# Substitution on 16-blocks, and a 32x32-matmul step to 32-blocks, in an rwkv scan on Trainium2

## The chip, the cores and the metric

One core of one Trainium2 chip runs the whole program. The metric is device time in microseconds (us) of one execution; the figure given for the kernel before is the median of its runs. The engines are PE (TensorE matmuls; PEld is its weight load), DVE (VectorE), ACT (ScalarE), POOL (GpSimd) and SP (SyncE, which here only issues DMAs).

## The reference

Two blocks follow each other on 512 tokens of width 1024. The first mixes a gated linear recurrence with dilated attention. The second has a latent of 512 and a context of 256 tokens; it merges pooling, a differential attention and an rwkv scan, and ends in a mixture of 32 experts. What the change touches is the rwkv scan, which runs over tokens in both directions, for 8 heads of 64:

```
def wkv_step(S, inp):
    r, w, k, v, a, b = inp
    sa = einsum('dbhvk,dbhk->dbhv', S, a)
    S = S * w[..., None, :] + sa[..., None] * b[..., None, :] + v[..., None] * k[..., None, :]
    return S, einsum('dbhvk,dbhk->dbhv', S, r)
```

The context is scanned first, in both directions, and its two final states start the scans of the latent. The expert stage reads 32 experts of three 1024x512 float32 matrices each.

## The kernel before, in words

**The scan in chunks.** The kernel does not step token by token. It takes chunks of 64 tokens. Inside a chunk, the effect of `a` and `b` on later tokens is a triangular 64x64 system for each head, and the inverse of its unit triangular matrix is needed. Between chunks only the 64x64 states are carried. There are 12 chunks (4 of the context, 8 of the latent) and 2 directions. A *batch* is two chunks of one direction, so there are 12 batches, taken alternately from the two directions (line 1319). A batch holds 2 chunks (`s`) x 4 feature tiles (`f`) x 2 heads per tile (`e`), which is 16 systems of 64x64.

**Phases of a batch.** `ph_a` (line 1128, once per chunk) loads the operands, forms decays with scans and exponentials, multiplies them into `AR` and `BK`, and puts the masked products into `AMB`. `ph_i` (line 1178) inverts the two 32x32 diagonal blocks of each of the 16 systems, 32 blocks in all: four DMAs bring the blocks to DRAM (`atD`), one brings them back as `LT`, laid out so that one of 32 blocks lies on each partition and each block is on four partitions. 31 steps of two DVE instructions (lines 1194 and 1196, tiles `Tm` and `Ti`) do the substitution; a partition holds 8 of the 32 rows of the inverse. Four DMAs store the result to `ttD`. `ph_b` (line 1201) loads it back with four DMAs into the diagonal blocks of `TT`, completes the 64x64 inverse with three groups of 32x32 matmuls through the PSUM tile `pi` (lines 1250 to 1262: a transposing matmul to get `T1`, a product `Qs`, a product into the off-diagonal block of `TT`, each evacuated by DVE for one half and ACT for the other), then applies the inverse (`px`, into `XV` or `XW`), forms the operands of the states (`pW`, evacuated into `WW`, lines 1282 to 1292), and carries the states through the two chunks (`pch`, `SI`, lines 1300 to 1312).

**Order.** The program is written as a list of calls; a planner then orders the instructions of each engine ahead of the run by their priorities and by its own estimates of their durations. On the chip each engine executes its list in order, so an instruction that waits holds up whatever is queued behind it on that engine, and this goes for DMA issues on SP too. `batch(n)` calls `ph_a` and `ph_i` of batch n, and then `ph_b` of batch n-2 (lines 1331 to 1338). Between the batches, projections of other branches are called as filler: `rw_prep` of the latent and `gate` in the first four batches, and after them the differential attention's q, k, v projections, the pool branch and more gates. All projections go through `load_chunk` (a DMA issued on SP, line 297, two buffers in this stage) and `split_chunk` (ACT `wh` line 304, POOL `wl` line 305, three buffers).

**Buffers.** PSUM in this stage has two banks for `mm` (projections), three for `aux` (`pta`, `pz0`, `pi`, `px`, and in `rw_prep` the lora products), one for `ch` and two for `pa` (`pA`, `ptb`, `pW`). `WW` has one buffer (`WWB = 1`), so the operands of the second chunk of a batch are written into the same place as those of the first. `AMB` has three buffers.

Of the kernel before, what the change touches and what calls it, by code (L numbers as in the profile page):

```python
# [9 lines left out]
F32 = mybir.dt.float32  # L10
# [3 lines left out]
ALU = mybir.AluOpType  # L14
# [25 lines left out]
def _consts():  # L40
    f = np.float32
    groups, off = {g: [] for g in "012345"}, {}
    where = {"bias1": "1", "invf": "1", "cos2": "3", "sin2": "3", "hsel": "5", "hbc": "5",
             "mask": "2", "tinit": "2", "sgn": "2",
             "iota32": "4", "tokid": "4", "tri": "4", "slot": "4", "tokrow": "4"}
# [59 lines left out]
    ti = np.zeros((4, 32, 8, 32))  # L105
    for g in range(4):
        for q in range(8):
            ti[g, :, q, 4 * q + g] = 1
    add("tinit", ti)
    return {"cst" + g: np.concatenate(v, 1) for g, v in groups.items()}, off  # L110


# [78 lines left out]
def _build(ctx, tc, A, out, dbg, upto):  # L191
# [901 lines left out]
    EARLY = ("kb", "kr", "cs", "ep", "em", "BK", "LT", "Ti", "Tm")  # L1093
# [6 lines left out]
    atD = [dp.tile([2, 2, 8, 32, 32], F32, name="atD%d" % i) for i in range(4)]  # L1100
    ttD = [dp.tile([2, 2, 8, 32, 32], F32, name="ttD%d" % i) for i in range(4)]
    yD = [dp.tile([128, 8, 4, 64], F32, name="yD%d" % d) for d in range(2)]
    par = ((0, E0), (1, E1))
    WWB = 1
    LATB, LPN = 10, (6, 5, 5, 3)

    def w1(name, shape=(4, 64), bufs=1, dt=F32):
# [12 lines left out]
    for d in range(2):  # L1120
        for e in range(2):
            t = rp.tile([128, 4, 64], F32, name="SI%d%d" % (d, e))
            GP.memset(t, 0.0)
            ir = slice(64, 128) if e == 0 else slice(0, 64)
            V.tensor_copy(t[ir], bc(ident[ir, None, ir], [64, 4, 64]))
            SI[d, e] = t

    def ph_a(d, c, s, AMB):

# [45 lines left out]
                          AF.Copy, scale=sgn[:, e:e + 1])  # L1175
        return AR, dec

    def ph_i(d, AMB, bi):

        for e in range(2):  # L1180
            for i in range(2):
                r0 = 64 * e + 32 * i
                SY.dma_start(atD[bi][e, i].rearrange("q s t -> s q t"),
                             AMB[r0:r0 + 32, e, :, :, 32 * i:32 * i + 32].rearrange("p s f t -> p (s f) t"))
        LT = w1("LT", (32, 32), 2)
        SY.dma_start(LT.rearrange("p s t -> p (s t)"),
                     atD[bi].rearrange("e i q s t -> (e i q) (s t)")[None].to_broadcast([4, 32, 1024]))
        T = w1("Ti", (8, 32), 2)
        SC.activation(T, tinit, AF.Copy)
        tmp = w1("Tm", (8, 32))  # L1190
        for s in (range(31) if d == 0 else range(31, 0, -1)):
            js, ts_ = (slice(0, s // 4 + 1), slice(s + 1, 32)) if d == 0 else (slice(s // 4, 8), slice(0, s))
            nj, n = js.stop - js.start, ts_.stop - ts_.start
            V.tensor_tensor(tmp[:, :nj, :n], bc(LT[:, s, None, ts_], [128, nj, n]),  # L1194
                            bc(T[:, js, s:s + 1], [128, nj, n]), ALU.mult)
            V.tensor_tensor(T[:, js, ts_], T[:, js, ts_], tmp[:, :nj, :n], ALU.add)  # L1196
        td = ttD[bi].rearrange("e i q (j g) t -> g (e i q) j t", g=4)
        for g in range(4):
            SY.dma_start(td[g], T[32 * g:32 * g + 32])

    def ph_b(d, chs, sts, AMB, bi):

        lat, c0 = chs[0] >= 4, min(chs)
        XE, XO = XV1 if lat and d else XV
        T = TT[d]
        fs = [(s, f) for s in range(2) for f in range(4)]
# [33 lines left out]
        c1, c2 = slice(32 * d, 32 * d + 32), slice(32 - 32 * d, 64 - 32 * d)  # L1240
        pi = ps("pi", "aux")
        T1, Qs = w1("T1", (2, 4, 32)), w1("Qs", (2, 4, 32))

        def evac(dst, src_):
            V.tensor_copy(dst[0], src_[0])
# [7 lines left out]
        for q, (s, f) in enumerate(fs):  # L1253
            for e in range(2):
                PE.matmul(col(pi, q, 32)[q2[e]], AMB[q1[e], e, s, f, c2], T1[q1[e], s, f, :], start=True,
                          stop=True, tile_position=(q1[e].start, q2[e].start))
        evac([Qs[q2[e]] for e in range(2)], [sf(pi, q2[e], 0, 32) for e in range(2)])
        for q, (s, f) in enumerate(fs):
# [63 lines left out]
    def run_b():  # L1322
        n, sts = pend.pop(0)
        ph_b(*sts)
        if n == 3 and dbg is not None and "S_c" in dbg:
            for d_ in range(2):
                for e, rows in par:
                    SY.dma_start(dbg["S_c"][128 * d_:128 * d_ + 128][rows, 256 * e:256 * e + 256],
                                 SI[d_, e][rows].rearrange("p a b -> p (a b)"))

    def batch(n):
        d, chs = batches[n]
        AMB = w1("AMB", (2, 2, 4, 192), 3)
        sts = {c - min(chs): ph_a(d, c, c - min(chs), AMB) for c in chs}
        ph_i(d, AMB, n % 4)
        pend.append((n, (d, chs, sts, AMB, n % 4)))
        if len(pend) > 2:
            run_b()

# [42 lines left out]
    for n in range(4, 12):  # L1382
        batch(n)
    while pend:
        run_b()
    if upto <= 2:
        return
# [742 lines left out]
```

## Time and profile before

| | |
|---|---|
| median of 3 runs | 1983.2 us (1969.72 to 1985.23) |
| the profiled execution's own time | 1981.57 us |
| its span, first to last instruction | 1979.7 us |
| mean granted TensorE clock | 0.934 |
| PE busy | 1755.4 us (89%) |
| DVE busy | 1091.5 us (55%) |
| ACT busy | 619.1 us (31%) |
| POOL busy | 526.5 us (27%) |

The span is what lies between the first and the last instruction. Busy times of different engines overlap. A busy PE is modelled, and its shares say little about how fast it works; the granted clock is a share of full speed. The scan's stage runs from about 535 us, when the first substitution begins, to about 1160 us. The experts' stage begins at about 1460 us and lasts to the end.

### The profile page before, as it was taken

To read this page: it belongs to the slowest core of one execution; us is meant where nothing else is said; L and a number is where in the kernel's file an instruction comes from. 1 tells how busy PE (TensorE), PEld (TensorE's weight loads), DVE (VectorE), ACT (ScalarE), POOL (GpSimd) and SP (SyncE) were. 2 spreads that over 40 slices of the span, in tenths; PEclk is the share of its full clock that TensorE was granted. 3 is DMA by queue.
4 is the path that set the end of the run, shared out by engine and by line. 5 is a ranking of instruction groups with operands and counts; after the bars stand their busy time and mean duration, and the time that the engine had idled before them with its cause. 6 is when DMAs were issued, how large, how long until landed. Compare 5 with 4: busy or idle time off the path is not lost. (4 is left out here: it accounts for less than half of the span.)

```text
span 1979.7 us, 31352 instructions
## 1 busy us (share of the span) xinstructions
PE 1755.4 (89%) x12309; PEld 1246.3 (63%) x12310; DVE 1091.5 (55%) x2364; ACT 619.1 (31%) x1164; POOL 526.5 (27%) x379
## 2 busy tenths in 40 slices
PE   6899998967787887888879998988979999999998
PEld 3874677953565776677667876677954545444544
DVE  4555675275487746777788655776342333332332
ACT  4234454443443222223333233443221111111110
POOL 2510337442335332231331132642310110101010
PEclk8999998988898898889898999999979999999999
DMA  8336513567546445445355338653629999999998
GB/s 298 108 111 218 197 64 103 195 181 250 156 121 171 135 137 122 109 109 137 99 151 152 81 112 280 204 179 111 246 99 387 387 386 386 386 387 386 386 386 289
DMA packets 275295, 415.89 MB, mean 210 GB/s; under 512 B 104876, under 2 KB 126408, under 8 KB 274888
## 3 DMA queue, kind: packets, MB, share of 16 engines
q1 hardware_dynamic: 246248, 383.44, 58.0%
q10 hardware_dynamic: 25568, 16.78, 2.8%
q0 software_dynamic: 3328, 13.63, 2.4%
q8 instruction: 98, 1.61, 0.3%
q14 instruction: 53, 0.43, 0.1%
HBM read 370.26 MB, written 43.53 MB: 209 GB/s over the span
## 5 line engine op out<-in xcount | busy, mean ns | idle before, releaser
L305 POOL TENSOR_TENSOR wl<-wr,wh 128x1024 fp32r<-128x1024 f32 x125 | 308.3, 2473 | 495.8 <-ACT wh L304 455.5
L304 ACT ACTIVATE wh<-wr 128x1024 fp32r<-128x1024 f32 x125 | 131.6, 1054 | 141.2 <-issue 54.9
L1980 POOL TENSOR_TENSOR yl<-ey,yh 128x512 fp32r<-128x512 f32 x30 | 38.4, 1279 | 466.1 <-ACT yh L1979 466.1
L310 PE MATMUL pf<-h2h,wh 128*128 128x512 f32 x344 | 147.8, 430 | 15.6 <-DVE Ti L1196 10.2
L1194 DVE TENSOR_TENSOR Tm<-LT,Ti 128x60 f32<-128x60 f32 (+24 forms) x372 | 116.8, 314 | 76.9 <-DMA LT<-atD 68.2
L311 PE MATMUL pf<-h2l,wh 128*128 128x512 f32 x344 | 144.5, 420 | 0.0
L312 PE MATMUL pf<-h2h,wl 128*128 128x512 f32 x344 | 143.3, 417 | 0.0
L1974 PE MATMUL ped<-wd,hid 128*64 128x512 f32 (+1 forms) x528 | 127.5, 585 | 0.7 <-ACT hid L1958 0.7
L1935 PE MATMUL peg<-wg,hTg 128*64 128x512 f32 x512 | 126.9, 597 | 0.0
L1942 PE MATMUL peu<-wu,hTg 128*64 128x512 f32 x512 | 125.3, 595 | 0.0
L1196 DVE TENSOR_TENSOR Ti<-Ti,Tm 128x60 f32<-128x60 f32 (+24 forms) x372 | 109.3, 294 | 9.1
L2007 DVE TENSOR_TENSOR acc<-acc,pcb 128x512 f32<-128x512 f32 (+1 forms) x124 | 76.0, 665 | 49.1 <-PE pcb L2006 49.0
L310 PEld LDWEIGHTS pf<-h2h,wh 128*128 128x128 f32 x344 | 69.4, 202 | 38.4 <-issue 15.4
L1974 PEld LDWEIGHTS ped<-wd,hid 128*64 128x64 f32 x528 | 39.9, 136 | 70.6 <-issue 65.9
L1942 PEld LDWEIGHTS peu<-wu,hTg 128*64 128x64 f32 x512 | 43.2, 137 | 65.1 <-issue 62.9
L311 PEld LDWEIGHTS pf<-h2l,wh 128*128 128x128 f32 x344 | 68.8, 200 | 18.5 <-issue 3.4
L1935 PEld LDWEIGHTS peg<-wg,hTg 128*64 128x64 f32 x512 | 41.9, 137 | 60.9 <-issue 58.1
L312 PEld LDWEIGHTS pf<-h2h,wl 128*128 128x128 f32 x344 | 68.6, 199 | 18.2 <-issue 2.1
L1282 PE MATMUL pW<-AMB,XV 128*128 128x64 f32 (+1 forms) x256 | 45.2, 335 | 28.7 <-DVE XV L1271 16.9
L1979 ACT ACTIVATE yh<-ey 128x512 fp32r<-128x512 f32 x30 | 18.9, 630 | 163.6 <-DVE ey L1978 90.2
L1915 DVE TENSOR_SCALAR hTg<-pg,gs,sh 128x128 f32<-128x128 f32 x64 | 25.3, 408 | 75.1 <-PE peu L1942 38.4
L1912 ACT ACTIVATE hTg<-pg,sh,gs 128x128 f32<-128x128 f32 x64 | 28.2, 457 | 121.4 <-PE peu L1942 55.4
(961 smaller groups left out, 4475.1 us busy)
## 6 DMA issues: line engine op xcount, KB each, us to landing
wg<-in_w_exp_gate_dram SPq DMA_DIRECT2D x64, 1024.0 KB
wu<-in_w_exp_up_dram SPq DMA_DIRECT2D x64, 1024.0 KB
wd<-in_w_exp_down_dram SPq DMA_DIRECT2D x62, 1024.0 KB
wr<-in_w_in_dram SPq DMA_DIRECT2D x97, 512.0 KB
kb<-kbD SPq DMA_DIRECT2D x24, 384.0 KB
wr<-in_w_out_dram SPq DMA_DIRECT2D x16, 512.0 KB
LT<-atD SPq DMA_DIRECT2D x12, 512.0 KB
thD<-mth ACTq DMA_DIRECT2D x24, 256.0 KB
```

Of the source, the lines that this page charges most:

```text
L304: SC.activation(hi, raw, AF.Copy)
L305: GP.tensor_tensor(lo, raw, hi.bitcast(F32), ALU.subtract)
L310: PE.matmul(p, ah, bh, start=start, stop=False)
L311: PE.matmul(p, ah, bl, start=False, stop=False)
L312: PE.matmul(p, al, bh, start=False, stop=stop)
L1194: V.tensor_tensor(tmp[:, :nj, :n], bc(LT[:, s, None, ts_], [128, nj, n]), bc(T[:, js, s:s + 1], [128, nj, n]), ALU.mult)
L1196: V.tensor_tensor(T[:, js, ts_], T[:, js, ts_], tmp[:, :nj, :n], ALU.add)
L1282: PE.matmul(pw[e][:, nw * f:nw * (f + 1)], X[:, s, f, :], AMB[:, e, s, f, n0:192], start=True, stop=True)
L1935: mm = PE.matmul(pg[64 * a:64 * a + 64, :], hT[:, k, 64 * a:64 * a + 64], gp[a][k // 4][:, k % 4, :], start=(k == 0), stop=(k == 7), tile_ ...
L1942: PE.matmul(pu[64 * a:64 * a + 64, :], hT[:, k, 64 * a:64 * a + 64], up[a][k // 4][:, k % 4, :], start=(k == 0), stop=(k == 7), tile_posit ...
L1974: PE.matmul(pd[64 * a:64 * a + 64, :], hid[:, m * k + 64 * a:m * k + 64 * a + 64], dn[q][a][:, k, 0:q1 - q0], start=(k == 0), stop=(k == 3 ...
L2007: V.tensor_tensor(acc[i][:, qs], acc[i][:, qs], p, ALU.add)
```

## The change

In `ph_i` the substitution is done on 16x16 diagonal blocks: 64 blocks in a batch, one on each partition and each block on two partitions, 15 steps instead of 31, and rows of 16 elements instead of 32. Eight DMAs instead of four take the blocks to DRAM, one DMA brings them back (1 KB per partition, before 4 KB), two instead of four store the result, and eight load it into the diagonal 16-blocks of a new tile `U` (three buffers, zeroed once). These loads are issued in `ph_i`; those of `ph_b` into `TT` are gone.

A new function `ph_m` joins two 16-blocks to a 32-block by four groups of 32 matmuls of 32x32: the transpose of `U`; the product of the `AMB` block with it, masked by `join` to the one off-diagonal 16-block; and the two products that give the off-diagonal part of the inverse and of its transpose. It uses two PSUM tiles of `aux`, one ACT evacuation and six DVE instructions. `ph_b` gets the transpose `T1` from it and no longer forms it with matmuls and evacuations. `ph_m` of a batch is called one batch later, after `ph_i` of the next batch, and ahead of the `ph_b` of the batch before it. `WW` gets two buffers.

```diff
+    join = cc("join").rearrange("p (d j) -> p d j", d=2)
+    eye = cc("eye32")
+    atD = [dp.tile([2, 4, 8, 16, 16], F32, name="atD%d" % i) for i in range(4)]
+    ttD = [dp.tile([2, 4, 8, 16, 16], F32, name="ttD%d" % i) for i in range(4)]
-    WWB = 1
+    WWB = 2
...
-    def ph_i(d, AMB, bi):
+    def ph_i(d, AMB, U, bi):
         for e in range(2):
-            for i in range(2):
-                r0 = 64 * e + 32 * i
+            for i in range(4):
+                r0 = 64 * e + 16 * i
                 SY.dma_start(atD[bi][e, i].rearrange("q s t -> s q t"),
-                             AMB[r0:r0 + 32, e, :, :, 32 * i:32 * i + 32].rearrange("p s f t -> p (s f) t"))
+                             AMB[r0:r0 + 16, e, :, :, 16 * i:16 * i + 16].rearrange("p s f t -> p (s f) t"))
-        LT = w1("LT", (32, 32), 2)
+        LT = w1("LT", (16, 16), 2)
...
-        for s in (range(31) if d == 0 else range(31, 0, -1)):
-            js, ts_ = (slice(0, s // 4 + 1), slice(s + 1, 32)) if d == 0 else (slice(s // 4, 8), slice(0, s))
+        for s in (range(15) if d == 0 else range(15, 0, -1)):
+            js, ts_ = (slice(0, s // 2 + 1), slice(s + 1, 16)) if d == 0 else (slice(s // 2, 8), slice(0, s))
             nj, n = js.stop - js.start, ts_.stop - ts_.start
             V.tensor_tensor(tmp[:, :nj, :n], bc(LT[:, s, None, ts_], [128, nj, n]),
                             bc(T[:, js, s:s + 1], [128, nj, n]), ALU.mult)
             V.tensor_tensor(T[:, js, ts_], T[:, js, ts_], tmp[:, :nj, :n], ALU.add)
-        td = ttD[bi].rearrange("e i q (j g) t -> g (e i q) j t", g=4)
-        for g in range(4):
-            SY.dma_start(td[g], T[32 * g:32 * g + 32])
+        td = ttD[bi].rearrange("e i q (j g) t -> g (e i q) j t", g=2)
+        for g in range(2):
+            SY.dma_start(td[g], T[64 * g:64 * g + 64])
+        for e in range(2):
+            for i in range(4):
+                r0, c0 = 64 * e + 16 * i, 16 * (i % 2)
+                SY.dma_start(U[r0:r0 + 16, :, c0:c0 + 16], ttD[bi][e, i].rearrange("q j t -> j q t"))
+
+    def b32(p, o, lhs, rhs):
+        for q in range(8):
+            for e, i, r in blocks:
+                PE.matmul(p[r, o + 32 * q:o + 32 * q + 32], lhs(r, q, e, i), rhs(r, q, e, i), start=True, stop=True,
+                          tile_position=(r.start, r.start))
+
+    def ph_m(d, AMB, U):
...
+        pt = ps("tit", "aux")
+        b32(pt, 0, lambda r, q, e, i: U[r, q], lambda r, q, e, i: eye[r])
+        T = w1("T16", (8, 32), 2)
+        SC.activation(T, q8(pt[:, 0:256]), AF.Copy)
+        b32(pt, 256, at, lambda r, q, e, i: T[r, q])
+        P = w1("PJ", (8, 32))
+        V.tensor_tensor(P, q8(pt[:, 256:512]), bc(join[:, d, None, :], [128, 8, 32]), ALU.mult)
+        pu = ps("tiu", "aux")
+        b32(pu, 0, lambda r, q, e, i: P[r, q], lambda r, q, e, i: U[r, q])
+        b32(pu, 256, lambda r, q, e, i: U[r, q], lambda r, q, e, i: P[r, q])
+        for e, i, r in blocks:
+            V.tensor_tensor(TT[d][r, :, :, 32 * i:32 * i + 32], U[r].rearrange("p (s f) t -> p s f t", s=2),
+                            pu[r, 0:256].rearrange("p (s f t) -> p s f t", s=2, f=4), ALU.add)
+        V.tensor_tensor(T, T, q8(pu[:, 256:512]), ALU.add)
+        return T
...
-        for e in range(2):
-            for i in range(2):
-                r0 = 64 * e + 32 * i
-                SY.dma_start(T[r0:r0 + 32, :, :, 32 * i:32 * i + 32].rearrange("p s f t -> p (s f) t"),
-                             ttD[bi][e, i].rearrange("q j t -> j q t"))
...
-                PE.matmul(col(pi, q, 32)[q1[e]], T[q1[e], s, f, c1], ident[q1[e], q1[e]], start=True, stop=True,
-                          tile_position=(q1[e].start, q1[e].start))
-        evac([T1[q1[e]] for e in range(2)], [sf(pi, q1[e], 0, 32) for e in range(2)])
...
+    def join_b():
+        for z in pend:
+            if len(z[1]) == 4 and (len(pend) == 1 or z is not pend[-1]):
+                d, _, _, AMB = z[1]
+                z[1] += (ph_m(d, AMB, U16[z[0] % 3]),)
...
+        ph_i(d, AMB, U16[n % 3], n % 4)
+        pend.append([n, (d, chs, sts, AMB)])
+        if len(pend) > 1:
+            join_b()
         if len(pend) > 2:
             run_b()
...
     while pend:
+        join_b()
         run_b()
```

## Rows read from the trace of the kernel before

**Rows 1.** Stage windows: length, then busy us by engine, granted clock, DMA share, GB/s

```profile
535.00:880.00 345.00, 292.28 (x2265) 231.25 (x2266) 243.22 (x617) 111.44 (x195) 120.04 (x105) 0.87 0.49 128
880.00:1130.00 250.00, 209.41 (x2590) 181.41 (x2590) 196.55 (x620) 82.03 (x164) 58.09 (x58) 0.90 0.48 126
1130.00:1200.00 70.00, 67.55 (x527) 53.12 (x521) 26.62 (x40) 22.81 (x36) 21.23 (x20) 0.98 0.47 152
...
1460.00:1980.00 520.00, 505.19 (x2658) 250.10 (x2657) 170.16 (x339) 67.37 (x129) 38.38 (x30) 0.99 0.99 364
```

**Rows 2.** Who waited for whom, DVE, 535 to 1130 us: total, times, longest

```profile
DVE Tm L1194 <- DMA LT<-atD: 68.2, 10, 11.0
...
DVE WW L1289 <- PE pch L1302: 3.0, 3, 1.6
DVE WW L1289 <- PE pch L1308: 2.0, 2, 1.6
```

**Rows 3.** Who waited for whom, PE, 535 to 880 us

```profile
PE px L1268 <- DVE TT L1245: 15.3, 3, 6.5
PE pf L310 <- DVE Ti L1196: 10.2, 2, 8.0
```

**Rows 4.** Who waited for whom, PE, 880 to 1130 us

```profile
PE pW L1282 <- ACT WW L1292: 19.7, 4, 6.5
PE pW L1282 <- DVE XV L1271: 9.7, 2, 6.9
```

**Rows 5.** The tile Ti: its instructions (ns min/median/max), and their busy sum by windows

```profile
L1194 DVE TENSOR_TENSOR Tm<-LT,Ti x372: 152/214/5960, 535.2 to 1124.5; 128x60 f32<-128x60 f32 x18, 128x54 f32<-128x54 f32 x12, 128x66 f32<-128x66 f32 x12, 128x28 f32<-128x28 f32 x12
L1196 DVE TENSOR_TENSOR Ti<-Ti,Tm x372: 127/212/5912, 538.2 to 1124.7; 128x60 f32<-128x60 f32 x18, 128x54 f32<-128x54 f32 x12, 128x66 f32<-128x66 f32 x12, 128x28 f32<-128x28 f32 x12
...
sum 1500.00, DVE 226.08 ACT 4.89; mean DVE 15.07 ACT 0.33
```

**Rows 6.** DVE and POOL in order of time: start, us, engine, line, what

```profile
916.60 0.20 DVE L1194 TENSOR_TENSOR Tm<-LT,Ti 128x35 f32<-128x35 f32 x1
...
918.63 0.17 DVE L1194 TENSOR_TENSOR Tm<-LT,Ti 128x16 f32<-128x16 f32 x1
...
884.96 2.30 DVE L1196 TENSOR_TENSOR Ti<-Ti,Tm 128x30 f32<-128x30 f32 x1
...
884.87 2.34 POOL L305 TENSOR_TENSOR wl<-wr,wh 128x1024 fp32r<-128x1024 f32 x1 [0.19 <-ACT wh L304]
```

**Rows 7.** DVE groups by shape, 500 to 1200 us: busy, mean ns, idle before

```profile
L1166 DVE TENSOR_TENSOR AMB<-pA,cst 128x256 f32<-128x256 f32 x16 | 6.3, 417 | 9.6 <-PE pA L1162 9.6
...
L1245 DVE COPY T<-pi 32x256 f32<-32x256 f32 x12 | 5.0, 413 | 3.6 <-PE pi L1250 3.4
```

**Rows 8.** ACT and PE in order of time

```profile
917.08 0.38 ACT L1443 ACTIVATE dk<-pt 128x256 f32<-128x256 f32 x1
...
937.14 0.69 PE L1250 MATMUL pi<-cst,TT 32*32 32x32 f32 x32
...
950.97 0.56 PE L1260 MATMUL pi<-TT,Qs 32*32 32x32 f32 x22
```

**Rows 9.** SP in order of time, DMA issues

```profile
913.76 2.07 SPq L1183 DMA_DIRECT2D atD<-AMB  x4
...
917.16 0.58 SPq L1186 DMA_DIRECT2D LT<-atD  x1
...
920.29 7.97 SPq L1199 DMA_DIRECT2D ttD<-Ti  x4
...
930.63 1.80 SPq L1213 DMA_DIRECT2D TT<-ttD  x4
...
963.27 0.56 SPq L1186 DMA_DIRECT2D LT<-atD  x1
```

**Rows 10.** Who waited for whom, 880 to 1130 us, SP and POOL

```profile
SPq L1213 <- DMA ttD<-Ti: 15.5, 8, 7.7
...
POOL wl L305 <- DMA TT<-ttD: 29.0, 1, 29.0
```

More of the change, by code (lines that the diff above doesn't have):

```diff
@@ L43, in _consts @@
     where = {"bias1": "1", "invf": "1", "cos2": "3", "sin2": "3", "hsel": "5", "hbc": "5",
-             "mask": "2", "tinit": "2", "sgn": "2",
+             "mask": "2", "tinit": "2", "join": "2", "eye32": "2", "sgn": "2",
              "iota32": "4", "tokid": "4", "tri": "4", "slot": "4", "tokrow": "4"}
@@ L104, in _consts @@
     add("sgn", sg)
-    ti = np.zeros((4, 32, 8, 32))
-    for g in range(4):
+    ti = np.zeros((2, 64, 8, 16))
+    for g in range(2):
         for q in range(8):
-            ti[g, :, q, 4 * q + g] = 1
+            ti[g, :, q, 2 * q + g] = 1
     add("tinit", ti)
+    jn = np.zeros((4, 32, 2, 32))
+    jn[:, 16:, 0, :16] = 1
+    jn[:, :16, 1, 16:] = 1
+    add("join", jn)
+    add("eye32", np.tile(np.eye(32), (4, 1)))
     return {"cst" + g: np.concatenate(v, 1) for g, v in groups.items()}, off
@@ L1092, in _build @@
     rpa, rpb = (cur["ctx"].enter_context(tc.tile_pool(name=n, bufs=1, reuse_waits="tile")) for n in ("b2i", "b2j"))
-    EARLY = ("kb", "kr", "cs", "ep", "em", "BK", "LT", "Ti", "Tm")
+    EARLY = ("kb", "kr", "cs", "ep", "em", "BK", "LT", "Ti", "Tm", "T16", "PJ")
     load_cst("2", cp2)
@@ L1099, in _build @@
     CW = 0.5 * math.exp(-0.5)
-    atD = [dp.tile([2, 2, 8, 32, 32], F32, name="atD%d" % i) for i in range(4)]
-    ttD = [dp.tile([2, 2, 8, 32, 32], F32, name="ttD%d" % i) for i in range(4)]
+    join = cc("join").rearrange("p (d j) -> p d j", d=2)
+    eye = cc("eye32")
+    atD = [dp.tile([2, 4, 8, 16, 16], F32, name="atD%d" % i) for i in range(4)]
+    ttD = [dp.tile([2, 4, 8, 16, 16], F32, name="ttD%d" % i) for i in range(4)]
     yD = [dp.tile([128, 8, 4, 64], F32, name="yD%d" % d) for d in range(2)]
     par = ((0, E0), (1, E1))
-    WWB = 1
+    WWB = 2
     LATB, LPN = 10, (6, 5, 5, 3)
@@ L1126, in _build @@
             SI[d, e] = t
+    U16 = []
+    for i in range(3):
+        t = rp.tile([128, 8, 32], F32, name="U16%d" % i)
+        GP.memset(t, 0.0)
+        U16.append(t)
     def ph_a(d, c, s, AMB):
@@ L1176, in ph_a @@
         return AR, dec
-    def ph_i(d, AMB, bi):
+    blocks = [(e, i, slice(64 * e + 32 * i, 64 * e + 32 * i + 32)) for e in range(2) for i in range(2)]
+    fs = [(s, f) for s in range(2) for f in range(4)]
+    def ph_i(d, AMB, U, bi):
         for e in range(2):
-            for i in range(2):
-                r0 = 64 * e + 32 * i
+            for i in range(4):
+                r0 = 64 * e + 16 * i
                 SY.dma_start(atD[bi][e, i].rearrange("q s t -> s q t"),
-                             AMB[r0:r0 + 32, e, :, :, 32 * i:32 * i + 32].rearrange("p s f t -> p (s f) t"))
-        LT = w1("LT", (32, 32), 2)
+                             AMB[r0:r0 + 16, e, :, :, 16 * i:16 * i + 16].rearrange("p s f t -> p (s f) t"))
+        LT = w1("LT", (16, 16), 2)
         SY.dma_start(LT.rearrange("p s t -> p (s t)"),
-                     atD[bi].rearrange("e i q s t -> (e i q) (s t)")[None].to_broadcast([4, 32, 1024]))
-        T = w1("Ti", (8, 32), 2)
+                     atD[bi].rearrange("e i q s t -> (e i q) (s t)")[None].to_broadcast([2, 64, 256]))
+        T = w1("Ti", (8, 16), 2)
         SC.activation(T, tinit, AF.Copy)
-        tmp = w1("Tm", (8, 32))
-        for s in (range(31) if d == 0 else range(31, 0, -1)):
-            js, ts_ = (slice(0, s // 4 + 1), slice(s + 1, 32)) if d == 0 else (slice(s // 4, 8), slice(0, s))
+        tmp = w1("Tm", (8, 16))
+        for s in (range(15) if d == 0 else range(15, 0, -1)):
+            js, ts_ = (slice(0, s // 2 + 1), slice(s + 1, 16)) if d == 0 else (slice(s // 2, 8), slice(0, s))
             nj, n = js.stop - js.start, ts_.stop - ts_.start
@@ L1196, in ph_i, with at, q8, ph_b @@
             V.tensor_tensor(T[:, js, ts_], T[:, js, ts_], tmp[:, :nj, :n], ALU.add)
-        td = ttD[bi].rearrange("e i q (j g) t -> g (e i q) j t", g=4)
-        for g in range(4):
-            SY.dma_start(td[g], T[32 * g:32 * g + 32])
-    def ph_b(d, chs, sts, AMB, bi):
+        td = ttD[bi].rearrange("e i q (j g) t -> g (e i q) j t", g=2)
+        for g in range(2):
+            SY.dma_start(td[g], T[64 * g:64 * g + 64])
[9 more added lines that the diff above has]
+    def ph_m(d, AMB, U):
+        def at(r, q, e, i):
+            return AMB[r, e, fs[q][0], fs[q][1], 32 * i:32 * i + 32]
+        def q8(ap):
+            return ap.rearrange("p (q t) -> p q t", q=8)
+        pt = ps("tit", "aux")
[13 more added lines that the diff above has]
+        return T
+    def ph_b(d, chs, sts, AMB, T1):
         lat, c0 = chs[0] >= 4, min(chs)
@@ L1205, in ph_b @@
         T = TT[d]
-        fs = [(s, f) for s in range(2) for f in range(4)]
         v3 = vTD[:, c0:c0 + 2].rearrange("t c (f e v) -> e t (c f) v", f=4, e=2)
@@ L1239, in ph_b @@
         q2 = [slice(64 * e + 32 - 32 * d, 64 * e + 64 - 32 * d) for e in range(2)]
-        c1, c2 = slice(32 * d, 32 * d + 32), slice(32 - 32 * d, 64 - 32 * d)
+        c2 = slice(32 - 32 * d, 64 - 32 * d)
         pi = ps("pi", "aux")
-        T1, Qs = w1("T1", (2, 4, 32)), w1("Qs", (2, 4, 32))
+        Qs = w1("PJ", (2, 4, 32))
         def evac(dst, src_):
@@ L1249, in ph_b @@
             for e in range(2):
-                PE.matmul(col(pi, q, 32)[q1[e]], T[q1[e], s, f, c1], ident[q1[e], q1[e]], start=True, stop=True,
-                          tile_position=(q1[e].start, q1[e].start))
-        evac([T1[q1[e]] for e in range(2)], [sf(pi, q1[e], 0, 32) for e in range(2)])
-        for q, (s, f) in enumerate(fs):
-            for e in range(2):
-                PE.matmul(col(pi, q, 32)[q2[e]], AMB[q1[e], e, s, f, c2], T1[q1[e], s, f, :], start=True,
+                PE.matmul(col(pi, q, 32)[q2[e]], AMB[q1[e], e, s, f, c2], T1[q1[e], q], start=True,
                           stop=True, tile_position=(q1[e].start, q2[e].start))
@@ L1334, in batch @@
         sts = {c - min(chs): ph_a(d, c, c - min(chs), AMB) for c in chs}
-        ph_i(d, AMB, n % 4)
-        pend.append((n, (d, chs, sts, AMB, n % 4)))
+        ph_i(d, AMB, U16[n % 3], n % 4)
+        pend.append([n, (d, chs, sts, AMB)])
+        if len(pend) > 1:
+            join_b()
         if len(pend) > 2:
```

## The prediction, made before the changed kernel ran

> **What bounds the kernel now.** I read the stages first [rows 1]. From 1460 us on the expert stage keeps PE busy for 505 of 520 us at a granted clock of 0.99 and the DMA engines at 0.99: nothing there is touched, and it can only start sooner. From 1130 to 1200 us PE is busy for 67.55 of 70 us. The scan's stage lies before that, and it looks different. In 880 to 1130 us DVE is busy for 196.55 of 250 us (79%), in 535 to 880 us for 243.22 of 345 (70%), while PE stands idle for 250 - 209.41 = 40.6 us and 345 - 292.28 = 52.7 us, at clocks of 0.90 and 0.87. So 93.3 us of PE idleness lies in the scan, and each us of it that goes should show at the end, since what follows starts when the scan's tiles are given back.
>
> Then I asked who makes PE wait. In both windows the long waits are on evacuations: `px` on DVE's copy into `TT` (15.3 us), a projection queued behind the substitution itself (10.2) [rows 3], `pW` on ACT's `WW` and on DVE's copy into `XV` (19.7 and 9.7) [rows 4]. The evacuations are late because DVE's list interleaves them with the substitution. The substitution is the largest single user of DVE: 744 instructions, 226.1 us [rows 5]. DVE itself mainly waits on one thing, `LT` (68.2 us in 10 waits) [rows 2]. A batch takes 963.27 - 917.16 = 46.1 us from one `LT` load to the next [rows 9], so 880 to 1130 us holds 5.4 batches, and the other 6.6 lie before or at the edges.
>
> **The change part by part.** *The substitution.* It falls from 62 to 30 instructions per batch, 744 to 360 in all. Their mean is now 226.1 / 744 = 0.304 us, their median about 0.213 [rows 5]. The new ones are 8 to 36 elements wide, and rows of such widths show 0.17 to 0.20 us [rows 6]; I take 0.18. The difference of mean and median, 0.091 us, comes from a few long ones. One took 2.30 us where its width asks 0.18, and POOL's `wl` split ran from 884.87 to 887.21, just across it [rows 6]. I let the long ones fall with the count: 360 x (0.18 + 0.091) = 97.6 us. The bounds are 360 x 0.18 = 65 us (none of them hit) and 360 x 0.304 = 109 us (they cost today's mean).
>
> The Trainium skill ("SBUF — State Buffer", the section "Who interferes with whom") says that a DVE instruction with two SBUF inputs and a GpSimd one that reads SBUF exclude each other, the later one blocking until the first ends. By that rule the long instructions are POOL's doing and not the substitution's, and the blocking may pass to another DVE instruction rather than fall with the count. It is the second case below.
>
> *The join on DVE.* `ph_m` adds six instructions per batch that read PSUM (the mask, four sums, the sum into `T`). The nearest rows are 0.417 us for 128x256 with a PSUM input and 0.413 for 32x256 [rows 7], so 6 x 0.417 x 12 = 30.0 us. `T1`'s copy goes: 12 x 0.413 = 5.0 us. DVE is left with 226.1 - 97.6 - 30.0 + 5.0 = 103.5 us less, 8.6 per batch (bounds 92 and 136 in all).
>
> *What of it reaches the end.* In 880 to 1130 us 5.4 x 8.6 = 46 us of DVE go. DVE is nearly the pace there but partly waits, so I take 60%: 28 us, under the 40.6 us that PE has to give. In the 6.6 other batches 57 us go; there the latent's projections and their splits also set the pace, and I take 40%: 23 us, under 52.7. Together 51 us. Late next is PE.
>
> *The join on PE.* 128 matmuls of 32x32 come per batch and 16 go: 1344 more. Such matmuls run at 0.69 / 32 = 22 ns apiece, once at 0.56 / 22 = 25 ns [rows 8]: 29 to 34 us. Part fills idle PE; about a third should not: 10 us (bounds 0 and 34). The join's ACT evacuation stands for that of `T1`, some 0.38 us each [rows 8]: nothing.
>
> *Two buffers of `WW`.* With one, DVE's `WW` for the second chunk waits for `pch` of the first: 3.0 + 2.0 us [rows 2]. I count 5 us. The 19.7 us that PE waits on ACT's `WW` [rows 4] look like the same thing, but `pW` waits for a PSUM bank of `pa`, of which there are still two; they are the upper bound (25 us together), zero is the lower.
>
> *DMAs on SP.* Four more stores to `atD`, four more loads back, two fewer stores to `ttD`: six issues of 0.45 to 0.52 us per batch [rows 9], about 3 us, 35 in all. On the way to `LT` lie only the four extra stores, 2.1 us. Against them `LT` brings 128 KB instead of 512: 384 KB take 3.0 us at the 126 GB/s of that window, 1.1 at the 364 GB/s of the last [rows 1]. Between 1.0 us lost and 0.9 won per batch I take nothing, and 12 us either way for the range. The loads into `U` move from `ph_b` to `ph_i`, behind the stores that they read. In the queue they already stand there: `TT`'s loads follow 2 us after `ttD`'s stores end [rows 9]. `ph_m` comes a batch later and has about 46 us of cover; without it, PE would see the wait for the stores, 15.5 / 8 = 1.9 us [rows 10], and four issues more.
>
> *Sum.* 51 - 10 + 5 = 46 us. The profiled execution took 1981.6 us, 1.6 less than the median, so 1981.6 - 46 + 1.6 = 1937 us.
>
> **The rivals.** *The blocking stays.* POOL's work is the same, so the 226.1 - 744 x 0.213 = 67.6 us of long instructions pass to others. DVE then saves only 158.5 - 65 - 25 = 69 us, and the 51 become 34: 34 - 10 + 5 = 29 us, 1954 us. For it speaks the pair of rows at 884.9 us; against it, that many other DVE instructions of this stage read PSUM. It is what the rule named above would have.
>
> *The join's hand-offs hold PE.* `ph_m` passes four times between PE and an evacuation, in two more tiles of the three `aux` banks. Today `px` behind `pi` waited three times, 5.1 us each [rows 3]. If six of the batches get one such wait, 31 of the 46 us go: 1968 us. Ten would give 1988. Against it speaks that `ph_m` does not hang on the states and can lie between projections.
>
> *The SP queue becomes the wait: slower.* After the substitution SP holds the stores (7.97 us in one batch), the 1.9 us until they land and eight loads of 0.45: 13.5 us, in which no projection weight can be issued. POOL once waited 29.0 us for a weight behind a `TT` load [rows 10]. It decides where the hold outlasts the chunks in stock; if half of the hold shows on PE in all batches, 81 us are added: 1937 + 81 = 2018 us. Against it: the stores and loads already stand together, and the two longest PE waits of either window are not on weights [rows 3, 4].
>
> *All idleness goes.* If PE loses its 93.3 us, 1981.6 - 93 = 1888 us, with the joins' matmuls paid by a clock nearer the 0.98 of the next window.
>
> *The second buffer does nothing*, because the bank decides: 5 us less, inside the first case.
>
> **How the numbers follow.** The forecast has 0.42 (its own range 1915 to 1958), the blocking 0.20, the hand-offs 0.18, the SP queue 0.13, all idleness 0.07. A measurement of this kernel can tell about 1%, 20 us, from no change. Below 1963 lie the forecast, the blocking and the full gain, less 0.03 for their edges: 0.66 faster. Within 1%: 0.18 + 0.03 = 0.21. Slower: 0.13. The range runs from 1888 to 1990 us: the full gain below, the hand-offs in ten batches above; most of the SP case and a little at each edge stay out.
>
> **What would show it.** The substitution's busy time should be 65 to 110 us in 360 instructions; well above that, the blocking was mis-sized. DVE's share in the scan's second half should fall from 79% to under 70% while batches come every 39 to 42 us instead of 46. The joins' groups of 32 matmuls should take 0.7 us, and PE should name `tit` or `tiu` in few waits; many, and the hand-offs have it. `TT` and `XV` waits of PE should halve; `WW`'s should stay if the bank decides. Projections that wait on `wl` behind `U`'s loads would show the SP case. I am wrong if batches still come every 46 us with DVE relieved: then something else, in the list's order or in the DMA round trip to `LT`, sets the pace.

## The result, and the profile after

The changed kernel takes **2007.2 us** (median of 4 runs, 2004.5 to 2013.0), against 1984.2 us for the kernel before in the same comparison: ratio **1.0141, 95% interval 1.0098 to 1.0184**, slower by 1.4%. The forecast was 1937 us, 2.3% faster.

First the stage windows of the changed kernel (columns as in [rows 1]), with one row more, from 480 us to the first scores matmul behind the scan:

```profile
535.00:880.00 345.00, 301.84 (x3539) 239.28 (x3538) 183.68 (x421) 103.29 (x185) 110.71 (x97) 0.85 0.45 115
880.00:1130.00 250.00, 209.22 (x3353) 182.82 (x3352) 148.22 (x409) 74.63 (x150) 61.90 (x60) 0.88 0.43 111
1460.00:1980.00 520.00, 497.83 (x2641) 247.17 (x2639) 176.44 (x359) 74.14 (x141) 45.12 (x33) 0.98 0.98 360
480.00:1231.00 751.00, 650.30 (x8263) 530.82 (x8263) 417.64 (x992) 236.06 (x433) 226.85 (x214) 0.88 0.44 118
```

And the last of these rows for the kernel before, whose scores begin 25 us earlier:

```profile
480.00:1206.00 726.00, 614.51 (x5575) 496.97 (x5576) 494.23 (x1316) 239.35 (x433) 225.21 (x211) 0.89 0.51 136
```

The whole loss lies in this stage: 751 - 726 = 25 us, and the spans differ by 2004.0 - 1979.7 = 24.3. In it DVE lost 77 us of work, as the change means it to, and PE's busy time grew by 36 us. PE's idle time, 111.5 us before, is still 100.7: DVE was relieved and PE hardly noticed.

The substitution of the changed kernel by its tile (columns as in [rows 5]) came out as forecast, 96.43 us of DVE in 360 instructions, where 97.6 were worked out:

```profile
L1211 DVE TENSOR_TENSOR Tm<-LT,Ti x180: 150/188/5095, 528.7 to 1141.9; 128x30 f32<-128x30 f32 x36, 128x14 f32<-128x14 f32 x24, 128x24 f32<-128x24 f32 x24, 128x15 f32<-128x15 f32 x12
...
sum 1500.00, DVE 96.43 ACT 3.60; mean DVE 96.43 ACT 3.60
```

But the batches do not come faster. The loads of `LT` in SP's order of time, changed kernel: four batches in 1084.77 - 876.40 = 208.4 us, 52.1 us each, where [rows 9] had 46.1:

```profile
876.40 0.53 SPq L1203 DMA_DIRECT2D LT<-atD  x1
...
1084.77 0.56 SPq L1203 DMA_DIRECT2D LT<-atD  x1
```

Over all 12 loads, from the first to the last (the two times behind the durations), it is 605 us against 567 for the kernel before:

```profile
L1203 SPq DMA_DIRECT2D LT<-atD x12: 528/532/581, 523.4 to 1128.8; - x12
```

```profile
L1186 SPq DMA_DIRECT2D LT<-atD x12: 556/557/613, 523.2 to 1090.5; - x12
```

Who waited for whom on DVE, 535 to 1130 us of the changed kernel (as [rows 2]). The wait for `LT` fell from 68.2 to 30.7 us (40.5 if the window runs on to 1200 us, where the last batch of the changed kernel lies), and what is late now comes mostly from PE:

```profile
DVE BK L1170 <- PE ptb L1185: 37.5, 9, 12.3
DVE WW L1330 <- PE pW L1323: 32.2, 19, 5.7
DVE Tm L1211 <- DMA LT<-atD: 30.7, 9, 6.3
```

The same on PE, 480 to 1231 us. The `pW` waits of [rows 4] are not among them any more; `pi` waits in their place, for `Qs` (in the buffers of `PJ`, from ACT) and for the `T` that `ph_m` leaves:

```profile
PE pi L1301 <- ACT PJ L1292: 24.6, 6, 7.9
PE pi L1296 <- DVE T L1250: 15.6, 5, 4.9
PE px L1309 <- DVE TT L1291: 9.9, 3, 8.8
PE tit L1226 <- DMA U<-ttD: 7.0, 8, 3.0
```

### The profile page after: what moved, and what is told of

It reads as the page before. It is cut to its first block, busy times and chain, and to the rows that moved or that the text cites. A ratio compares the mean times of both kernels' runs of the same rounds, so it can differ in the third digit from the quotient of the medians.

```text
span 2004.0 us, 36536 instructions
## 1 busy us (share of the span) xinstructions
PE 1787.5 (89%) x14997; PEld 1275.4 (64%) x14998; DVE 1012.5 (51%) x2040; ACT 616.4 (31%) x1164; POOL 528.2 (26%) x382
## 5 line engine op out<-in xcount | busy, mean ns | idle before, releaser
L317 PE MATMUL pf<-h2l,wh 128*128 128x512 f32 x344 | 149.1, 433 | 0.0
L2058 DVE TENSOR_TENSOR acc<-acc,pcb 128x512 f32<-128x512 f32 (+1 forms) x124 | 75.8, 665 | 40.5 <-PE pcb L2057 40.3
L1211 DVE TENSOR_TENSOR Tm<-LT,Ti 128x15 f32<-128x15 f32 (+4 forms) x180 | 55.9, 311 | 45.4 <-DMA LT<-atD 40.5
L317 PE MATMUL pt<-wl,h2h 128*128 128x256 f32 x192 | 61.1, 318 | 0.0
L316 PE MATMUL pt<-wh,h2h 128*128 128x256 f32 x192 | 60.6, 315 | 0.3 <-DVE dql L1525 0.3
```

The lines of the kernel that those rows point to most:

```text
L316: PE.matmul(p, ah, bh, start=start, stop=False)
L317: PE.matmul(p, ah, bl, start=False, stop=False)
L2058: V.tensor_tensor(acc[i][:, qs], acc[i][:, qs], p, ALU.add)
```

## Experiments

Ratios are to the kernel before, with 95% intervals; where two other kernels are compared, the difference of their ratios is taken times 1983 us. An edit also lets the planner order the remaining instructions anew. Run 8 shows what a new order alone can do: 3 to 4 us in the kernels without the join, 25 to 27 us in the changed kernel.

**1. DVE's relief alone** (`sub15`). 15 of the 31 steps; the rest of each 32-block's inverse is left out.

```diff
-        for s in (range(31) if d == 0 else range(31, 0, -1)):
+        for s in (range(15) if d == 0 else range(31, 16, -1)):
```

> The kernel before with only 15 of the 31 steps of each substitution (the other 16 steps are left out, so the inverse is incomplete); joins, DMAs and buffers as before. DVE loses 384 of 744 substitution instructions, about 110 us of its 226. Theory H (PE's own issue time and the hand-offs between engines set the scan's pace, DVE's load does not): PE's idle time between 480 us and the first scores falls by less than 20 us, the time stays within 1% of before, 1965 to 2000 us. Theory R (DVE's relief is worth the 51 us that was predicted, and the change loses it and more elsewhere): 1930 to 1945 us.

Measured: 1973.1 us, 0.996 [0.9938, 0.9982]. In the stage DVE fell from 494 to 391 us, a relief as large as the one on which the forecast rests, and 8 us came of it. DVE's share was not the pace.

**2. The same with a smaller `LT`** (`sub15_small_lt`).

```diff
-                     atD[bi].rearrange("e i q s t -> (e i q) (s t)")[None].to_broadcast([4, 32, 1024]))
+        LT = w1("LT", (256,), 2)
+        SY.dma_start(LT, atD[bi].rearrange("e i q s t -> (e i q) (s t)")[None, :, 0:256].to_broadcast([4, 32, 256]))
...
-            V.tensor_tensor(tmp[:, :nj, :n], bc(LT[:, s, None, ts_], [128, nj, n]),
+            V.tensor_tensor(tmp[:, :nj, :n], bc(LT[:, None, 8 * (s % 16):8 * (s % 16) + n], [128, nj, n]),
```

> The kernel before with 15 of the 31 substitution steps, as in the run of that alone, and LT loaded with 1 KB per partition instead of 4 KB, of which the steps read arbitrary overlapping pieces (a part of the inverse is left out, and what is computed is of no use). The number of instructions and their shapes stay those of the run with 15 steps, which gave 1973.1 us and in which DVE waited 100.9 us for LT in 12 waits (8.4 per batch; 36.4 in 11 in the kernel without the join). If the round trip of LT is what held the relief back, the waits fall to about 40 us and the time to 1915 to 1940 us (0.966 to 0.979). If it is hidden by other work, 1965 to 1980 us (0.991 to 0.999), and the gain of the kernel without the join comes from something else.

Measured: **1906.1 us, 0.9648 [0.9608, 0.9687]**: (0.996 - 0.9648) x 1983 = 62 us from a load of 128 KB in place of 512; count and shapes of the instructions are those of run 1. DVE's wait for `LT`, 480 to 1200 us, first with 15 steps alone, then with the small load:

```profile
DVE Tm L1194 <- DMA LT<-atD: 100.9, 12, 11.5
```

```profile
DVE Tm L1193 <- DMA LT<-atD: 23.6, 10, 6.3
```

The first row shows where the relief of run 1 went: the shorter substitution was followed by a longer wait, 100.9 us where there had been 68.2. The two differ by 77.3 us, and the stage is 58 us shorter (PE busy 606.22 of 713 us against 590.33 of 655):

```profile
480.00:1193.00 713.00, 606.22 (x5568) 494.98 (x5567) 391.37 (x927) 234.52 (x428) 221.86 (x209) 0.89 0.52 138
```

```profile
480.00:1135.00 655.00, 590.33 (x5575) 480.44 (x5576) 400.34 (x932) 238.54 (x433) 230.08 (x214) 0.93 0.53 147
```

**3. The change without the join** (`no_join`). `ph_m` without matmuls: `T` by a DVE transpose, `TT` a copy of `U`; the off-diagonal 16-blocks of the inverse are left at zero.

```diff
-        b32(pt, 0, lambda r, q, e, i: U[r, q], lambda r, q, e, i: eye[r])
...
+        V.transpose(T.rearrange("p q t -> p (q t)"), U.rearrange("p q t -> p (q t)"))
...
+            V.tensor_copy(TT[d][r, :, :, 32 * i:32 * i + 32], U[r].rearrange("p (s f) t -> p s f t", s=2))
```

> The changed kernel with the join's matmuls left out: the off-diagonal 16-blocks stay zero, TT gets a DVE copy of U and T1 a DVE transpose of it. Short substitution, its DMAs and two buffers of WW stay. Theory H (the join's matmuls and their hand-offs on PE are what the change loses; the second WW buffer is its only real gain, about 28 us, and the short substitution gives about 8): 1984 - 28 - 8 and a few us for the transposing matmuls that are gone, 1935 to 1955 us. Rival D (the new DMAs or the new plan of the other instructions cost, not the join): 1975 us or more.

Measured: **1913.7 us, 0.9691 [0.9642, 0.9741]**, 61 us faster than the kernel before. The rest of the change is a clear gain, and the join costs (1.0141 - 0.9691) x 1983 = **89 us**. The stage row, and four batches in 946.50 - 810.05 = 136.5 us, 34.1 each:

```profile
480.00:1142.00 662.00, 590.00 (x5188) 479.65 (x5186) 407.58 (x980) 231.40 (x417) 231.29 (x217) 0.91 0.50 139
```

```profile
810.05 0.55 SPq L1203 DMA_DIRECT2D LT<-atD  x1
...
946.50 0.53 SPq L1203 DMA_DIRECT2D LT<-atD  x1
```

Against the changed kernel's stage, 89 us longer, PE is busy 60 us longer and idle 29 us longer. Of the 60 us, the join's matmuls are 44.3 (each row's time until the next one starts or it ends itself, summed over `tit` and `tiu`); the rest is other work at a granted clock of 0.88 instead of 0.91.

**4. One buffer of `WW`**, with the join (`one_ww`) and without it (`no_join_one_ww`; the same blocks at zero).

```diff
-    WWB = 2
+    WWB = 1
```

> The changed kernel with one buffer of WW again. If the second buffer frees only DVE and the PSUM banks of pW decide: within 6 us of the changed kernel, 2001 to 2013 us. If it carries a gain that the joins hide: 15 to 30 us slower than changed, 2020 to 2037 us.

> no_join (join's matmuls left out, the off-diagonal 16-blocks stay zero) with one buffer of WW. If the second buffer is worth the same here as in the changed kernel (28 us): 1936 to 1950 us. If it pays only where the joins crowd PE and the short substitution alone is what gains: within 10 us of no_join, 1905 to 1924 us. If the gain of no_join is nearly all the buffer's: 1965 to 1985 us.

Measured: 1.0287 [1.0237, 1.0337] and 0.9669 [0.9638, 0.97]. The second buffer is worth 29 us with the join and nothing without it. The forecast's 5 us describe neither. What it takes away are DVE's waits for `pch`, as the prediction had it: with one buffer and the join, 480 to 1251 us,

```profile
DVE WW L1330 <- PE pch L1349: 30.7, 6, 8.4
...
DVE WW L1330 <- PE pch L1343: 9.0, 3, 4.9
```

and none with two. Without the join the same waits of the one buffer are 11.5 and 6.8 us, and cost nothing at the end.

**5. The join twice** (`join_twice`): each of its four groups is issued twice.

```diff
-        for q in range(8):
+        for q in list(range(8)) * 2:
```

> The changed kernel with each group of the join's 32x32 matmuls issued twice into the same place (same values), 128 more matmuls per batch; hand-offs, DVE and DMAs as changed. Theory H: PE's issue time adds up in full, the four groups cost about 44 us of PE now, so 30 to 50 us more than the changed kernel, 2037 to 2057 us. Rival W (only the hand-offs of the join cost, the matmuls fill PE's idle time): under 12 us more, 2005 to 2019 us.

Measured: 1.0588 [1.0535, 1.0642], 89 us for the second copy, as much as the first had cost. The second copy adds no evacuation and no PSUM tile, so neither is needed for the price, and its own issue is 32 us (`tit` and `tiu` 76.6 instead of 44.3). PE's idle time in the stage grows by 49 us; 21.8 us of it stand before `tiu` with no wait that the trace shows.

**6. The join issued, but read by nothing** (`join_unread`, `join_unread_after_b`): the kernel of run 3 with the four groups on `U`, `AMB` and the identity, called ahead of `ph_b` and behind it.

```diff
+        pt, pu = ps("tit", "aux"), ps("tiu", "aux")
+        b32(pt, 0, lambda r, q, e, i: U[r, q], lambda r, q, e, i: eye[r])
+        b32(pt, 256, at, lambda r, q, e, i: U[r, q])
+        b32(pu, 0, lambda r, q, e, i: U[r, q], lambda r, q, e, i: U[r, q])
+        b32(pu, 256, lambda r, q, e, i: U[r, q], at)
```

> no_join with the four groups of 32 join matmuls issued again, but on U, AMB and the identity alone and with nothing reading their results: PE's issue time of the join without its hand-offs (the join itself stays left out, the off-diagonal 16-blocks are zero). The changed kernel is 93 us above no_join. If issue time and clock are the price: 60 to 90 us above no_join, 1975 to 2005 us. If the hand-offs through ACT and DVE are: 30 to 50 us above, 1944 to 1964 us.

> The kernel without the join (off-diagonal 16-blocks of the inverse left at zero) with the join's four groups of matmuls issued on other data and read by nothing, as before, but the groups called behind the applying phase of the older batch instead of ahead of it. Called ahead they cost 121 us over the kernel without them (2034.6 against 1913.7). If the place in PE's list is what makes them dear (the older batch's chain of small products stands behind 128 matmuls), 1955 to 1975 us: 40 to 60 us over the kernel without them, near the 44 to 46 us of their own issue, with PE's wait of pi on the evacuation into PJ (46.2 us in 8) gone. If their issue in this stage is dear wherever it stands, 2015 to 2035 us.

Measured: 1.0297 [1.0264, 1.0329] and 1.0314 [1.0274, 1.0353], so 120 and 124 us over run 3. A price made only by the join's hand-offs, or only by the place of the call, is refuted: matmuls that nobody reads cost no less, in either place. The stage rows, ahead and behind, show 66.5 and 82.1 us more of PE work than run 3, of which 46.4 and 44.6 are the groups themselves, at a clock of 0.88 and 0.84, and 58.5 and 57.9 us more of idleness:

```profile
480.00:1267.00 787.00, 656.51 (x8263) 541.17 (x8264) 416.34 (x980) 234.33 (x421) 235.23 (x218) 0.88 0.43 120
```

```profile
480.00:1282.00 802.00, 672.06 (x8263) 551.44 (x8264) 400.20 (x980) 235.13 (x421) 234.65 (x218) 0.84 0.43 117
```

**7. Half the join's matmuls** (`join_dve_t`, and with the call behind `ph_b`, `join_dve_t_after_b`): DVE transposes in place of the first group and of one of the two last ones.

```diff
+        V.transpose(T.rearrange("p q t -> p (q t)"), U.rearrange("p q t -> p (q t)"))
...
-        b32(pu, 0, lambda r, q, e, i: P[r, q], lambda r, q, e, i: U[r, q])
...
+            V.transpose(TT[d][r, :, :, 32 * i:32 * i + 32], T[r].rearrange("p (s f) t -> p s f t", s=2))
```

> The changed kernel with two of the join's four matmul groups and its ACT evacuation replaced by DVE transposes of 32x32 blocks (one of 128x256, four of 32x256); one PSUM tile instead of two. PE loses about 22 us of issue time, DVE keeps its count. Theory H: 15 to 30 us less than the changed kernel, 1977 to 1992 us. Rival W (hand-offs cost): one hand-off to PE and back less per batch, but DVE ones in their place, 1995 to 2010 us.

> The changed kernel with two of the four join groups and their evacuations replaced by DVE transposes, and the join called behind the applying phase of the older batch. The two edits alone gave 1981.8 us (0.9992) and 1980.1 us (1.0014) against 2007 for the changed kernel. If the join's price has two separate parts, the number of matmuls that PE issues (half of them gone, about 25 us) and the place of the call in the planner's list (about 27 us), they add: about 1955 us, ratio 0.986, and the stage from 480 us to the first scores matmul falls from 751 us to about 708, with the granted clock at 0.90 or more. If both edits took away the same thing, namely evacuations of the join that stand ahead of those of the older batch in the lists of DVE and ACT, the second adds little: 1975 to 1982 us, ratio 0.996 to 1.0.

Measured: 0.9992 [0.9966, 1.0017] and 1.0023 [1.0, 1.0046]. Half of the groups away is worth 30 us with the call ahead. With the call behind it is worth nothing: the whole join in that place (run 8) has 1.0014, and its stage is the shorter one, 728 us against 742, at a granted clock of 0.91 against 0.87. So the price does not go with the number of matmuls; why, these runs do not show.

**8. The order alone**, all work kept: the changed kernel with the join called behind `ph_b` (`join_after_b`); and with `ph_b` called ahead of `ph_i` in the kernel before (`before_b_early`), in run 3 (`no_join_b_early`) and in the changed kernel (`after_b_early`, where the join stands behind `ph_b` as well).

```diff
-        if len(pend) > 1:
-            join_b()
         if len(pend) > 2:
             run_b()
+        if len(pend) > 1:
+            join_b()
```

> The changed kernel with ph_m of batch n-1 called behind ph_b of batch n-2 instead of ahead of it, so that the states' chain comes first for the planner. If the place of the join among the hand-offs matters: 10 to 25 us less, 1982 to 1997 us. If PE's issue time is what counts: within 8 us of the changed kernel, 1999 to 2015 us.

> The kernel before with one call moved: the applying phase of batch n-2 is called ahead of the substitution of batch n instead of behind it. The work is the same to the instruction. If a changed call order merely draws another schedule from the planner, this moves the time by some 10 to 30 us in either direction. If the kernel before is insensitive to it, the ratio is within 0.995 to 1.005, and the 27 us that the same kind of move gave the changed kernel belong to the join.

> The kernel without the join (off-diagonal 16-blocks of the inverse left at zero), with the same move of the call. If its 64 us below the kernel before are a property of the work, it stays within 1900 to 1935 us (0.96 to 0.978). If they were a lucky schedule, it comes to 1950 us or more.

> The changed kernel with the same move: the applying phase of batch n-2, then the substitution of batch n, then the join of batch n-1. If the join called ahead of the applying phase is what cost 27 us, this is near 1980 us (0.995 to 1.005). If the place only scatters the time, it may fall anywhere from 1975 to 2035 us, and the three orders of the changed kernel (2007, 1980 and this) give the scatter; either way it should lie at least 45 us above the kernel without the join in the same order.

Measured: 1.0014 [0.999, 1.0039], then 1.0016 [0.9989, 1.0043], 0.9711 [0.9657, 0.9765] and 1.0005 [0.9979, 1.0032]. The kernels without a join barely move (3 and 4 us). With the join behind, the changed kernel is 25 to 27 us faster in both orders; but half a join (run 7) and an unread one (run 6) gain nothing by the same move, so what holds the changed kernel's first order back belongs to its own chain of waits and is not settled. In the second order the join still costs (1.0005 - 0.9711) x 1983 = **58 us**, give or take 12 by the intervals. The stage rows of that order, without and with the join, differ by 47 us, 19 of PE's work and 28 of its idleness; the join's matmuls are 38.7 us there, so PE's other work took some 20 us less, at a granted clock of 0.91 instead of 0.89:

```profile
480.00:1160.00 680.00, 602.98 (x5215) 488.50 (x5211) 404.17 (x982) 233.56 (x423) 233.58 (x218) 0.89 0.50 139
```

```profile
480.00:1207.00 727.00, 621.82 (x8265) 510.91 (x8264) 410.74 (x993) 237.41 (x433) 232.37 (x218) 0.91 0.48 130
```

**9. Parts put into the kernel before.** `T1` by DVE transposes (`before_t`); two `WW` buffers, paid for with one buffer of `LT` (`before_two_ww`), and with the transposes too (`before_two_ww_t`); transposes and two `WW` buffers, paid for with single buffers of `kr` and `Ti` and with `Qs` in the place of `T1` instead (`before_t_two_ww`).

```diff
-                PE.matmul(col(pi, q, 32)[q1[e]], T[q1[e], s, f, c1], ident[q1[e], q1[e]], start=True, stop=True,
-                          tile_position=(q1[e].start, q1[e].start))
-        evac([T1[q1[e]] for e in range(2)], [sf(pi, q1[e], 0, 32) for e in range(2)])
...
+            V.transpose(T1[q1[e]], T[q1[e], :, :, c1])
```

> The kernel before with T1 formed by DVE transposes instead of 16 matmuls and two evacuations per batch. Theory H: 5 to 15 us less than before, 1969 to 1979 us. Rival: within 4 us of before.

> The kernel before with two buffers of WW, the space taken from LT (one buffer instead of two); the 32-block substitution as it was. Theory H: the second WW buffer is worth 15 to 30 us on its own, less up to 10 us of DVE waiting for LT: 1955 to 1975 us. Rival B (the PSUM banks of pW decide, and the 28 us seen in the changed kernel came from its own plan): 1980 to 1995 us.

> As before_two_ww, and T1 in ph_b formed by two DVE transposes instead of 16 matmuls and two evacuations per batch. Theory H (PE's issue time and hand-offs count, DVE has room): 5 to 15 us under before_two_ww. Rival: DVE is the pace, within 4 us of it or slower.

> before_t (32-block substitution, T1 by DVE transposes) with two buffers of WW, the space taken from kr and Ti (one buffer each) and from Qs (in T1's place); LT keeps two. If the second WW buffer gains by itself: 10 to 25 us under before_t, 1942 to 1957 us. If it gains only with the short substitution, or what gives up its buffer costs more: 1965 to 1995 us.

Measured: 0.9955 [0.9931, 0.9978], 1.0222 [1.0179, 1.0265], 1.0171 [1.0127, 1.0216] and 0.9985 [0.9962, 1.0009]. One buffer of `LT` instead of two costs 44 us that the second `WW` does not make up for; DVE's wait for `LT` is 91.1 us there, 68.2 before. `before_t` is the one complete kernel that is faster than both beyond its interval, 9 us below the kernel before.

## Why the prediction was wrong

The join was priced far too low, and that turned the sign. What the rest of the change gives came out near its forecast by luck: 61 us without the join (run 3), where 51 + 5 = 56 were worked out, though the relief of DVE was put too high and the load of `LT` at nothing. With the join's 89 us it makes 61 - 89 = -28.

**The join on PE: the step that failed.** It was put at 10 us, by the words that "about a third should not" fit into idle PE. Its issue was nearly right (the last section says why the rate behind it was not): in the changed kernel's order of time a group that runs undivided takes about 0.7 us as forecast,

```profile
961.20 0.69 PE L1226 MATMUL tit<-cst,U 32*32 32x32 f32 x58 [1.14 <-DMA U<-ttD]
```

and all 48 groups took 44.3 us, 37.3 net of the `T1` group that left `pi`, against 29 to 34. Wrong was what it does to the end: 58 to 89 us by order (runs 3 and 8), each time more than its issue, and 120 us with nothing depending on it (run 6). The idle time of PE in the scan was not a store into which this work could be put: idleness grew by 28 to 58 us when it was added (runs 3, 5, 6 and 8). My reading, which no run shows by itself: PE executes a fixed list, its idle moments lie where a product of the chain is not ready, and 128 matmuls more in each batch's list put off the next member of the chain instead of filling those moments. Through which waits the idleness grows changes from order to order (in run 6, with the call ahead, `pi` waits 46.2 us on `PJ`; with the call behind 0.2, and there `ptb` waits 25.2 on `AMB` and `px` 19.1 on `TT`), the granted clock of the stage moves with it, and half the matmuls can cost as much as all (run 7). Why the price is what it is stays open.

**What of DVE's relief reaches the end.** 51 us were forecast by a share of 60% and 40%. DVE's 103 us bring 8 us by themselves (run 1). That the package without the join still brought 61 has a reason that the prediction had weighed and put at nothing:

**The load of `LT`.** "Between 1.0 us lost and 0.9 won per batch I take nothing." Those bounds set 1.1 to 3.0 us for the smaller load against 2.1 for four more stores. The smaller load alone was worth 62 us (run 2), 5.2 per batch. The bound took the rate of all transfers in the window, 126 GB/s, for the rate of this one; the last section shows what it was. It shows too that the change's own load takes longer than that of run 2, 5.8 us against 3.5, so the 62 us are not the share of `LT` in the 61 of run 3; that share was not measured. The row that should have led here was in [rows 2]: DVE's largest wait, 68.2 us in 10, named `LT`, and I read DVE's share in its place. Run 2 cuts the load with the short substitution only; the small load with all 31 steps was not tried, and what each of the two is worth may depend on which comes first.

**Two buffers of `WW`**: 5 us forecast, 29 with the join and 0 without (run 4). The mechanism was right and the size was not: with the join the waits of `WW` for `pch` are 39.7 us. PE's 19.7 us of waits on ACT's `WW` [rows 4] are gone from the changed kernel, but they are 1.3 us in the one with a single buffer too, so it was not the second buffer that took them away. Whether the PSUM bank decides was not tested.

**The rivals.** *Join's hand-offs*: `tit` and `pi` do wait, 24.6 + 15.6 + 7.0 = 47.2 us in the stage, but run 6 costs more without any hand-off of the join. *The blocking stays*: with a median of 0.186 us, 360 instructions would be 67 us, so 29 of 96.43 are long ones; they fell with the count, from 67.6. *The SP queue*: run 3 has the same DMAs and is 61 us faster, and in the changed kernel PE waits 0.5 us on `wl` in the whole stage, so that is not why it came out slower. *All idleness goes* had the joins' matmuls paid by a faster clock; the stage's clock went from 0.89 to 0.88. None of my slower cases had the price in PE's own list, and "I am wrong if batches still come every 46 us with DVE relieved" was the sentence that came true.

## What to carry to other kernels

An engine that is idle for 15% of a latency-bound stage has no room to give away: price added instructions there at their whole issue or more, and test it by issuing them with nothing reading them (here that test gave 120 us where the join cost 58 to 89, so it warns and does not measure). Before relieving a busy engine, read what it itself waits for, and try cutting that wait first; here nearly half of the arithmetic behind one DMA load was worth 8 us, and then three quarters of that load 62. For a DMA that an engine waits for, look at the DMA share while it is alone, not at the mean rate of the stage.

## What the runs showed of the hardware

**A broadcast load uses few DMA engines.** In the kernel with 15 steps, whose `LT` load is that of the kernel before, the DMA rows of 995 to 1003 us in 40 slices (busy tenths of 16 DMA engines, then GB/s) and the instruction that waited for it:

```profile
DMA  9433322332222222222222211111111000000000
GB/s 266 154 102 102 123 92 102 133 102 72 87 87 97 77 82 82 113 77 97 113 82 113 82 72 72 51 51 41 61 41 51 20 31 0 0 0 0 0 0 0
```

```profile
999.34 0.19 DVE L1194 TENSOR_TENSOR Tm<-LT,Ti 128x31 f32<-128x31 f32 x1 [8.68 <-DMA LT<-atD]
```

The load was issued 10.5 us earlier (9.7 to 12.1 in the last six batches). In the changed kernel the same stretch, from the issue to the first instruction that waited, is 5.8 us (5.7 to 6.4); in the kernel of run 2 it is 3.5 (3.4 to 4.0). SP's row of the kernel with 15 steps, then SP's and DVE's of the two others:

```profile
988.89 0.59 SPq L1186 DMA_DIRECT2D LT<-atD  x1
```

```profile
936.72 0.53 SPq L1203 DMA_DIRECT2D LT<-atD  x1
...
942.50 0.17 DVE L1211 TENSOR_TENSOR Tm<-LT,Ti 128x15 f32<-128x15 f32 x1 [2.15 <-DMA LT<-atD]
```

```profile
948.76 0.57 SPq L1186 DMA_DIRECT2D LT<-atD  x1
...
952.21 0.19 DVE L1193 TENSOR_TENSOR Tm<-LT,Ti 128x31 f32<-128x31 f32 x1 [2.17 <-DMA LT<-atD]
```

The last two bring the same 128 KB, with two copies in the broadcast and with four. Now the share of the engines. In the kernel with 15 steps, once the other transfers are through, at about 995.5 us, what is left of the load runs at two to three tenths, mostly two, of the DMA engines and some 90 GB/s; in the experts' stage they all move 364 GB/s [rows 1]. In the changed kernel, 939 to 943 us, it is one tenth and 41 to 61 GB/s:

```profile
DMA  2121000000111111111111111111110000000000
GB/s 82 51 41 20 0 20 20 0 0 20 61 41 41 61 41 61 41 41 61 41 41 61 41 41 61 41 61 41 41 41 0 0 0 0 0 0 0 0 0 0
```

The Trainium skill has the rule in its page "DMA: Bandwidth & Descriptors", section "Rules for kernel authors": a leading broadcast dimension of c copies confines the whole DMA to at most c of the 16 engines. The traces agree: four copies, 0.2 to 0.3 where 4/16 is 0.25; two copies, 0.1 where 2/16 is 0.125. The same section's remedy, an outermost dimension that is a multiple of 16, was not tried here; if four times as many engines took the 512 KB, it might give the kernel before much of run 2's gain without the change, which no run here shows.

**A float32 matmul of this kernel has two rows in the trace.** The changed kernel's 32 matmuls in each of 12 groups are 384, and are listed as

```profile
L1226 PE MATMUL tit<-cst,U x768: 184/191/258, 550.9 to 1171.2; 32*32 32x32 f32 x192
```

So the 0.69 us of [rows 8] were 16 matmuls on two 32-row blocks of the array, not 32, and the 0.69 us above 29 matmuls on four. The two errors in my rate, the count and the number of blocks, nearly cancelled.
